# Group norm's product and transposition moved behind the state's renewal in a pooling and RWKV-7 block

## The chip, the cores and the metric

The kernel runs on one core of one Trainium2 chip. The metric is the device time of one execution in microseconds (us), as a median over executions. The engines are TensorE (PE for matmuls, PEld for its weight loads), VectorE (DVE), ScalarE (ACT), GpSimd (POOL) and SyncE (SP), whose queue issues all of the kernel's DMAs.

## What is computed

One layer for a sequence of 4096 tokens with 1024 features. A normalised and modulated input goes through one projection; half of its outputs feed a pooling mixer, the other half an RWKV-7 recurrence with 8 heads of 64; both are gated, put side by side and projected again. The part that matters here is the recurrence and the group norm behind it:

```
def step(S, inp):
    r_t, w_t, k_t, v_t, am_t, b_t = inp
    sa = jnp.einsum('bhij,bhj->bhi', S, am_t)
    S = (S * w_t[:, :, None, :]
         + sa[..., None] * b_t[:, :, None, :]
         + v_t[..., None] * k_t[:, :, None, :])
    y = jnp.einsum('bhij,bhj->bhi', S, r_t)
    return S, y
...
mu = jnp.mean(yh, axis=-1, keepdims=True)
var = jnp.mean(jnp.square(yh - mu), axis=-1, keepdims=True)
yh = (yh - mu) * lax.rsqrt(var + GN_EPS)
yh = yh * ln_w[l].reshape(H, N) + ln_b[l].reshape(H, N)
bonus = jnp.sum(rh * kh * r_k[l].reshape(H, N), axis=-1, keepdims=True) * vh
y_rwkv = (yh + bonus).reshape(B, T, D_RWKV) * jax.nn.silu(z)
```

## The kernel before

Stage one (to about 450 us) prepares the weights and does the pooling half. Stage two handles the recurrence in 16 blocks of 256 tokens, each of four chunks of 64 tokens. A block has three parts, written one behind the other: `scores` (L649) multiplies the chunks' vectors with each other on PE (L663), masks the products on DVE (L670) and copies the diagonal blocks on ACT (L678); `inverse` (L698) turns them over on DVE (L709), scales them and inverts small triangular matrices with some sixty dependent products and sums on DVE (L727, L732); `chain` (L796) walks through the four chunks one after the other. Stage three, the output projection (`project`, L924), runs within and behind the last block.

For one chunk `chain` does this, each step waiting for the one before: PE multiplies the state S with the chunk's vectors (L815); ACT copies the result to xa (L822); PE applies the inverse (L827) and beside it starts the next chunk's sum (`lead`, L790); ACT copies that to UV (L835); PE multiplies it with BT (L843 before, L842 after), which DVE adds to the decayed state: the renewal of S, four products of DVE (L849 before, L848 after; the decay Sd is L839 before, L838 after). Behind it PE finishes the chunk's output (L854), and ACT copies that to y (L861). PE is in order over all of this.

The projections of the next block (`front`, L537: f16 products L557 to L559, their ACT and DVE steps at L561, L562 and behind, the scan L596 among them) are cut into small steps. `fill(n)` issues n of them, so that PE has independent products to do while the chain waits. In the last block the fill is stage three.

The group norm works on two chunks at once, as a generator of three steps: `run(gns[0], 1)` issues one step, `run(gns[0])` all that are left. Step one squares y (ACT, L871), sums (DVE, L873, L874) and takes the power on POOL (L876); step two multiplies y by the result (DVE, L878, called the product below); step three, `gn_out`, transposes y on PE (L890, four transpositions into the tile ytp), scales on ACT (L892, four activations), adds and multiplies on DVE (L893, L894) and stores mx (SP, L896). The first half's steps are issued within the chain, those of the second half in the next block's scores.

The written order isn't the final one. A scheduler orders each engine's instructions by priority, which follows the written order; the products of the chain on PE are kept in their order (`ordered`), and copies and renewals of the chain are raised by 400 places (`tc.high_priority(offset=PRI)`).

Of the kernel before, what the change touches and what calls it, by code (L numbers as in the profile page):

```python
# [52 lines left out]
def kernel(  # L53
# [426 lines left out]
    with ExitStack() as ph:  # L480
# [289 lines left out]
        def ordered(mm):  # L770

            pin[0] = True
            return tc.keep_in_program_order(mm)
# [22 lines left out]
        def chain(b, f, fill):  # L796
            AR, UV, sc, BT, pc = f["AR"], f["UV"], f["sc"], f["BT"], f["pc"]
            MT = UV[0:64].rearrange("q c (h t) -> q (c h) t", h=NH)
            pe, po = f["px"]
            uo = 4 * HS  # L800
            for ch in range(NCH):
                par = 256 * (ch % 2)

                psn = ps_s.tile([P, 512], F32, tag="psn", name=f"psn{b}_{ch}")
                if ch % 2 == 0:
                    y = blk.tile([P, 512], F32, tag="y", name=f"y{b}_{ch}", bufs=3)
                yv = y[64 * (ch % 2) : 64 * (ch % 2) + 64].rearrange("q (j f e) -> q j f e", f=2, e=HS)
                uv = UV[0:64, ch, :].rearrange("q (j f e) -> q j f e", f=2, e=HS)

                for p in range(NPAIR):  # L810
                    cs = slice(par + p * HS, par + (p + 1) * HS)
                    for ar in range(2):
                        for hf, px in ((0, pe), (1, po)):
                            o, ro = 64 * hf, 64 * (hf ^ ar)
                            ordered(PE.matmul(  # L815
                                px[ro : ro + 64, cs], AR[o : o + 64, p, ch, ar, :], S[o : o + 64, p, :],
                                start=(p == 0 and ar == 1), stop=(ar == 0), skip_group_check=True,
                            ))
                xa = blk.tile([64, 2, 256], F32, tag="W", name=f"xa{b}_{ch}")
                for hf, px in ((0, pe), (1, po)):  # L820
                    with tc.high_priority(offset=PRI):
                        A.copy(xa[:, hf, :], px[64 * hf : 64 * hf + 64, par : par + 256])  # L822
                fill(FA)
                nl = lead(b, f, ch + 1) if ch + 1 < NCH else iter(())
                for p in range(NPAIR):
                    for hf in range(2):
                        ordered(PE.matmul(  # L827
                            psn[64 * hf : 64 * hf + 64, uo + p * HS : uo + (p + 1) * HS],
                            MT[:, ch * NH + 2 * p + hf, :], xa[:, hf, p * HS : (p + 1) * HS],
                            start=True, stop=True, skip_group_check=True,  # L830
                        ))
                    run(nl, 1)
                for hf in range(2):
                    with tc.high_priority(offset=PRI):
                        A.copy(uv[:, :, hf], psn[64 * hf : 64 * hf + 64, uo:].rearrange("q (j e) -> q j e", e=HS))  # L835
                run(gns[0], 1)

                Sd = blk.tile([P, NPAIR, HS], F32, tag="Wt", name=f"Sd{b}_{ch}")  # L838
                V.tensor_mul(Sd, S, pc[:, :, ch : ch + 1].to_broadcast([P, NPAIR, HS]))  # L839
                fill(FB)  # L840
                for h in range(NH):
                    o, e = 64 * (h % 2), slice(h * HS, (h + 1) * HS)  # L842
                    ordered(PE.matmul(  # L843
                        psn[o : o + 64, (h // 2) * HS : (h // 2 + 1) * HS], BT[:, ch, e], UV[:, ch, e],
                        start=True, stop=True, skip_group_check=True,
                    ))
                with tc.high_priority(offset=PRI):
                    for p in range(NPAIR):  # L848
                        V.scalar_tensor_tensor(  # L849
                            S[:, p, :], psn[:, p * HS : (p + 1) * HS], pc[:, p, ch : ch + 1], Sd[:, p, :], op0=ALU.mult, op1=ALU.add,  # L850
                        )
                for h in range(NH):
                    hf, o = h % 2, 64 * (1 - h % 2)
                    ordered(PE.matmul(  # L854
                        (pe, po)[hf][o : o + 64, par + (h // 2) * HS : par + (h // 2 + 1) * HS],
                        sc[:, ch * NH + h, 64:128], UV[:, ch, h * HS : (h + 1) * HS],
                        start=False, stop=True, skip_group_check=True,
                    ))
                for hf, px in ((0, pe), (1, po)):
                    o = 64 * (1 - hf)  # L860
                    A.copy(yv[:, :, hf], px[o : o + 64, par : par + 256].rearrange("q (j e) -> q j e", e=HS))  # L861
                run(gns[0])
                if ch % 2 == 1:
                    gns[0] = gn(b, f, ch // 2, y)
                    run(gns[0], 1)
                fill(FY)

        def gn(b, f, j, y):
            bon, szt = f["bon"], f["szt"]
            ysq = blk.tile([P, 512], F32, tag="y", name=f"ysq{b}_{j}", bufs=3)  # L870
            A.activation(ysq, y, AF.Square)  # L871
            var = sm.tile([P, NH], F32, tag="var", name=f"var{b}_{j}")
            V.tensor_reduce(var, ysq.rearrange("q (h j) -> q h j", h=NH), axis=AX.X, op=ALU.add)  # L873
            V.tensor_scalar(var, var, 1.0 / HS, GN_EPS, op0=ALU.mult, op1=ALU.add)  # L874
            rstd = sm.tile([P, NH], F32, tag="rstd", name=f"rstd{b}_{j}")
            G.tensor_tensor(rstd, var, nhalf[:, :NH], op=ALU.pow)  # L876
            yield
            V.tensor_mul(  # L878
                y.rearrange("q (h j) -> q h j", h=NH), y.rearrange("q (h j) -> q h j", h=NH),
                rstd.unsqueeze(2).to_broadcast([P, NH, HS]),  # L880
            )
            yield
            gn_out(b, f, j, y)
# [32 lines left out]
        def run(g, n=100000):  # L916
            for _ in range(n):
                if next(g, run) is run:
                    return
# [48 lines left out]
        gns = [iter(())]  # L968
# [84 lines left out]
```

## Time and profile before

| what | us |
|---|---|
| median of three executions | 2112.47 |
| lowest, highest | 2110.7, 2113.29 |
| the profiled execution | 2114.03 |
| its span, first to last instruction | 2112.3 |
| mean granted clock of TensorE, as a share | 0.984 |

The profiled execution is 1.56 us above the median, and 1.7 us of it lie outside the span. The profile's times count from the start of the span. One row of a timeline is an instruction, or several alike; the brackets at its end give the idle time of the engine ahead of it and what ended it.

### The profile page before, as it was taken

To read this page: it belongs to the slowest core of one execution; us is meant where nothing else is said; L and a number is where in the kernel's file an instruction comes from. 1 tells how busy PE (TensorE), PEld (TensorE's weight loads), DVE (VectorE), ACT (ScalarE), POOL (GpSimd) and SP (SyncE) were. 2 spreads that over 40 slices of the span, in tenths; PEclk is the share of its full clock that TensorE was granted. 3 is DMA by queue.
4 is the path that set the end of the run, shared out by engine and by line. 5 is a ranking of instruction groups with operands and counts; after the bars stand their busy time and mean duration, and the time that the engine had idled before them with its cause. 6 is when DMAs were issued, how large, how long until landed. Compare 5 with 4: busy or idle time off the path is not lost.

```text
span 2112.3 us, 48406 instructions
## 1 busy us (share of the span) xinstructions
PE 1979.8 (94%) x20186; PEld 1460.1 (69%) x20186; DVE 1404.4 (66%) x3533; ACT 1045.7 (50%) x2247; POOL 130.8 (6%) x262
## 2 busy tenths in 40 slices
PE   5999999999999999999999999999999989999998
PEld 2444444687777777777777777777777767788886
DVE  7898987466857757668577676685675766533333
ACT  3555433355565565655655656556556553322211
POOL 0000000000000000000000000000000000100000
PEclk8999999999999999999999999999999999999999
DMA  8867767200110110101101101011011334433422
GB/s 311 277 224 240 241 216 271 68 21 2 32 32 2 31 27 7 32 4 30 32 2 31 27 7 32 3 30 32 2 31 31 131 112 139 165 136 133 155 96 74
DMA packets 140445, 183.20 MB, mean 87 GB/s; under 512 B 12097, under 2 KB 94017, under 8 KB 140226
## 3 DMA queue, kind: packets, MB, share of 16 engines
q1 hardware_dynamic: 140226, 180.11, 25.9%
q8 instruction: 158, 2.59, 0.5%
q14 instruction: 61, 0.50, 0.1%
HBM read 121.22 MB, written 58.85 MB: 85 GB/s over the span
## 4 chain that ended last, share of the span: by engine, by line
PE 47%; DVE 31%; ACT 13%; issue 4%; DMA 2%; POOL 1%; SPq 0%; ACTq 0%; DVEq 0%; POOLq 0%
PE po L953 6%; PE po L955 6%; PE po L954 6%; DVE Wt L727 5%; DVE W L732 4%; PE pp L412 4%; PE pp L411 4%; PE pp L410 4%; PE pj L557 3%; PE pj L558 2%; PE pj L559 2%; DVE sc L670 2%; PE scp_sc L663 2%; DVE L L596 2%; ACT UV L678 2%
## 5 line engine op out<-in xcount | busy, mean ns | idle before, releaser
L557 PE MATMUL pj<-hh,w2h 128*128 128x257 f16 x2176 | 604.3, 278 | 14.3 <-DVE kS L562 13.5
L559 PE MATMUL pj<-hh,w2l 128*128 128x257 f16 x2176 | 598.1, 275 | 0.0
L558 PE MATMUL pj<-hl,w2h 128*128 128x257 f16 x2176 | 596.6, 274 | 0.0
L557 PEld LDWEIGHTS <-w2h 128*128 128x128 f16 x2176 | 213.1, 98 | 69.1 <-issue 27.4
L558 PEld LDWEIGHTS <-w2h 128*128 128x128 f16 x2176 | 215.6, 99 | 47.8 <-issue 17.0
L559 PEld LDWEIGHTS <-w2l 128*128 128x128 f16 x2176 | 211.7, 97 | 31.7
L953 PE MATMUL po<-wo,mh 128*128 128x512 f32 x512 | 204.6, 400 | 2.4 <-ACT mh L937 2.4
L954 PE MATMUL po<-wo,mh 128*128 128x512 f32 x512 | 202.1, 395 | 0.0
L411 PE MATMUL pp<-lo,w1h 128*128 128x512 f16 x512 | 194.0, 379 | 1.4 <-DVE lo L225 1.4
L410 PE MATMUL pp<-hi,w1h 128*128 128x512 f16 x512 | 194.1, 380 | 0.6 <-ACT hi L224 0.6
L412 PE MATMUL pp<-hi,w1l 128*128 128x512 f16 x512 | 194.0, 379 | 0.0
L957 DVE TENSOR_TENSOR x<-po,x 128x512 f32<-128x512 f32 x64 | 44.2, 691 | 155.8 <-PE po L955 155.7
L959 ACT ACTIVATE sq<-x 128x512 f32<-128x512 f32 x64 | 40.4, 631 | 212.0 <-DVE x L957 194.9
L727 DVE TENSOR_TENSOR Wt<-W,Ab 128x30 f32<-128x30 f32 (+7 forms) x480 | 118.5, 247 | 13.7 <-ACT Ab L711 3.1
L732 DVE TENSOR_TENSOR W<-W,Wt 128x30 f32<-128x30 f32 (+7 forms) x480 | 117.9, 246 | 8.8
L953 PEld LDWEIGHTS po<-wo,mh 128*128 128x128 f32 x512 | 97.0, 189 | 24.6 <-ACT mh L937 2.6
L954 PEld LDWEIGHTS po<-wo,mh 128*128 128x128 f32 x512 | 96.8, 189 | 22.2
L678 ACT COPY UV<-sc 32x256 f32<-32x256 f32 x128 | 81.5, 637 | 48.4 <-DVE sc L670 46.3
L955 PE MATMUL po<-wo,ml 128*128 128x512 f32 x256 | 101.6, 398 | 0.0
L562 DVE SCALAR_TENSOR_TENSOR kS<-pj,c,kS 128x256 f32<-128x256 f32 x64 | 30.2, 471 | 103.4 <-ACT kS L561 102.9
L412 PEld LDWEIGHTS <-w1l 128*128 128x128 f16 x512 | 50.1, 98 | 61.6 <-issue 2.0
L410 PEld LDWEIGHTS <-w1h 128*128 128x128 f16 x512 | 50.2, 98 | 59.0 <-issue 0.8
(244 smaller groups left out, 3815.1 us busy)
## 6 DMA issues: line engine op xcount, KB each, us to landing
x<-in_x_dram SPq DMA_DIRECT2D x64, 256.0 KB, 3.1
out_dram<-x SPq DMA_DIRECT2D x64, 256.0 KB, 2.0
xk<-in_xT_dram SPq DMA_DIRECT2D x56, 256.0 KB, 4.1
xt<-in_x_dram SPq DMA_DIRECT2D x28, 512.0 KB, 5.7
wada<-in_w_ada_dram SPq DMA_DIRECT2D x24, 512.0 KB, 6.7
w2raw<-in_w_in_dram SPq DMA_DIRECT2D x17, 512.0 KB, 6.0
hh<-hT_hi SPq DMA_DIRECT2D x32, 257.0 KB, 4.1
hl<-hT_lo SPq DMA_DIRECT2D x32, 257.0 KB, 3.3
```

What stands on the lines that cost most here:

```text
L410: PE.matmul(pp, w1_hi[m][:, k, :], hi, start=(k == 0), stop=False)
L411: PE.matmul(pp, w1_hi[m][:, k, :], lo, start=False, stop=False)
L412: PE.matmul(pp, w1_lo[m][:, k, :], hi, start=False, stop=(k == KT - 1))
L557: unpin(PE.matmul(pp, w2_hi[m][:, k, :], hh[k], start=(k == 0), stop=False))
L558: PE.matmul(pp, w2_hi[m][:, k, :], hl[k], start=False, stop=False)
L559: PE.matmul(pp, w2_lo[m][:, k, :], hh[k], start=False, stop=(k == KT - 1))
L678: A.copy(stg[o : o + 32, :, i8], sc[o : o + 32, i8, o : o + 32].rearrange("q i t -> q t i"))
L727: V.tensor_mul(tmp[:, :n, :k], W[:, r0:, k : k + 1].to_broadcast([P, n, k]), Ab[:, k : k + 1, :k].to_broadcast([P, n, k]),)
L732: V.tensor_add(W[:, r0:, :k], W[:, r0:, :k], tmp[:, :n, :k])
L953: unpin(PE.matmul(po, mh[:, k, ts_], wo[0][k][n], start=(k == 0), stop=False))
L954: PE.matmul(po, mh[:, k, ts_], wo[1][k][n], start=False, stop=False)
L955: PE.matmul(po, (ml[:, k] if b % 2 == 0 else ml[k])[:, ts_], wo[0][k][n], start=False, stop=(k == KT - 1))
```

## The change

The call for step two of the first half moves, in every chunk, from behind the copies L835 to behind the renewal of S. The call for the rest, which ran at the end of each chunk, now stands only in the second and fourth chunk, ahead of the next half's start. So of the first half (chunks one and two), step two is issued in the third chunk behind the renewal, and step three, instead of at the end of the third chunk, in the fourth behind its renewal.

```diff
@@ -833,7 +833,6 @@
                 for hf in range(2):
                     with tc.high_priority(offset=PRI):
                         A.copy(uv[:, :, hf], psn[64 * hf : 64 * hf + 64, uo:].rearrange("q (j e) -> q j e", e=HS))
-                run(gns[0], 1)
 
                 Sd = blk.tile([P, NPAIR, HS], F32, tag="Wt", name=f"Sd{b}_{ch}")
                 V.tensor_mul(Sd, S, pc[:, :, ch : ch + 1].to_broadcast([P, NPAIR, HS]))
@@ -849,6 +848,7 @@
                         V.scalar_tensor_tensor(
                             S[:, p, :], psn[:, p * HS : (p + 1) * HS], pc[:, p, ch : ch + 1], Sd[:, p, :], op0=ALU.mult, op1=ALU.add,
                         )
+                run(gns[0], 1)
                 for h in range(NH):
                     hf, o = h % 2, 64 * (1 - h % 2)
                     ordered(PE.matmul(
@@ -859,8 +859,8 @@
                 for hf, px in ((0, pe), (1, po)):
                     o = 64 * (1 - hf)
                     A.copy(yv[:, :, hf], px[o : o + 64, par : par + 256].rearrange("q (j e) -> q j e", e=HS))
-                run(gns[0])
                 if ch % 2 == 1:
+                    run(gns[0])
                     gns[0] = gn(b, f, ch // 2, y)
                     run(gns[0], 1)
                 fill(FY)
```

On DVE, in the third chunk of a block (the numbers are buffers), this stands from the second renewal to the third in the changed kernel:

```order
L848 SCALAR_TENSOR_TENSOR S<-psn_1_5199,pc_3683,Sd_1_5246 128x64 x4
L838 TENSOR_TENSOR Sd_2_5358<-S,pc_3683 128x256
L873 TENSOR_REDUCE var_0_5288<-ysq_0_5286 128x8
L874 TENSOR_SCALAR var_0_5288<-var_0_5288 128x8
L878 TENSOR_TENSOR y_0_5105<-y_0_5105,rstd_0_5291 128x512
L596 SCALAR_TENSOR_TENSOR L_3_5262<-rst,tw_3_5260 128x256
L608 SCALAR_TENSOR_TENSOR AR_4333<-kS_13_5162,vec,Ppad_3665 128x4x64
L606 SCALAR_TENSOR_TENSOR tb_3_5395<-ta_3_5261,kS_13_5162 128x256
L611 TENSOR_TENSOR AR_4333<-rS_14_5257,Ppad_3665 128x4x64
L609 SCALAR_TENSOR_TENSOR BK_4572<-tb_3_5395,pv,Pi_3_5263 128x4x64
L610 TENSOR_TENSOR ta_3_5261<-ta_3_5261,kS_13_5162 128x256
L848 SCALAR_TENSOR_TENSOR S<-psn_2_5300,pc_3683,Sd_2_5358 128x64 x4
```

The kernel before has these twelve in the same order: the product L878 did not move on its engine.

On DVE, from the third renewal to the fourth (mx is the tile of step three, vS a projection of the next block):

```order
-L615 SCALAR_TENSOR_TENSOR rk_3_5417<-rS_14_5257,pv,ta_3_5261 128x256
-L839 TENSOR_TENSOR Sd_3_5462<-S,pc_3683 128x256
-L893 TENSOR_TENSOR mx_0_5390<-mx_0_5390,bon_3681 128x512
-L562 SCALAR_TENSOR_TENSOR vS_15_5405<-pj_15_5293,c_103,vS_15_5405 128x256
-L894 TENSOR_TENSOR mx_0_5390<-mx_0_5390,szt_3682 128x512
-L849 SCALAR_TENSOR_TENSOR S<-psn_3_5423,pc_3683,Sd_3_5462 128x64 x4
+L562 SCALAR_TENSOR_TENSOR vS_15_5392<-pj_15_5293,c_103,vS_15_5392 128x256
+L615 SCALAR_TENSOR_TENSOR rk_3_5404<-rS_14_5257,pv,ta_3_5261 128x256
+L838 TENSOR_TENSOR Sd_3_5449<-S,pc_3683 128x256
+L848 SCALAR_TENSOR_TENSOR S<-psn_3_5410,pc_3683,Sd_3_5449 128x64 x4
+L893 TENSOR_TENSOR mx_0_5470<-mx_0_5470,bon_3681 128x512
+L894 TENSOR_TENSOR mx_0_5470<-mx_0_5470,szt_3682 128x512
```

L893 and L894 moved from ahead of the fourth renewal to behind it, where L562 of zS, L873, L620, L874 and the first mask L670 follow in this order (before, L873, L562, L874, the mask and then L620 did). On ACT the four L892 moved in the same way, from behind the third chunk's copies L861, ahead of the copies L822, to behind the fourth chunk's copies L835, ahead of its L861.

On PE, around the fourth chunk's product with BT (scp is the next block's score product), before:

```order
L557 LDWEIGHTS w2h_2179
L557 MATMUL pj_16_5419<-hh_1_4329,w2h_2179 128x257
L558 LDWEIGHTS w2h_2179
L558 MATMUL pj_16_5419<-hl_1_4331,w2h_2179 128x257
L559 LDWEIGHTS w2l_2180
L559 MATMUL pj_16_5419<-hh_1_4329,w2l_2180 128x257
L663 MATMUL scp_0_sc<-AR_4333,BK_4572 128x128
L843 MATMUL psn_3_5423<-UV_3684,BT_4310 64x64 x8
L854 MATMUL px_0_5007<-UV_3684,sc_4309 64x64
```

and now:

```order
L557 LDWEIGHTS w2h_2179
L557 MATMUL pj_16_5406<-hh_1_4329,w2h_2179 128x257
L558 LDWEIGHTS w2h_2179
L558 MATMUL pj_16_5406<-hl_1_4331,w2h_2179 128x257
L559 LDWEIGHTS w2l_2180
L559 MATMUL pj_16_5406<-hh_1_4329,w2l_2180 128x257
L890 MATMUL ytp_0_5469<-ident,y_0_5105 128x128
L842 MATMUL psn_3_5410<-UV_3684,BT_4310 64x64 x8
L890 MATMUL ytp_0_5469<-ident,y_0_5105 128x128 x3
L854 MATMUL px_0_5007<-UV_3684,sc_4309 64x64
```

The transpositions L890 stood one ahead of the third chunk's L843 and three behind its L854; there an f16 product (L557) has taken the first one's place. Fifteen blocks are changed alike. In the last block the first half's four transpositions move to behind the fourth chunk's L842, and the second half's four to five output products later. On SP the store L896 of the first half now stands behind the next three loads of hh and hl instead of ahead of them, and POOL's order is the same.

## Rows read from the trace of the kernel before

**Rows 1.** The page: its head and part 1.

```profile
span 2112.3 us, 48406 instructions
...
PE 1979.8 (94%) x20186; PEld 1460.1 (69%) x20186; DVE 1404.4 (66%) x3533; ACT 1045.7 (50%) x2247; POOL 130.8 (6%) x262
```

**Rows 2.** The chain of waits from 604 to 692 us: start, length, what.

```profile
625.32 1.40 ACT mx L892 x4
...
630.58 1.24 DVE Ab L709
...
663.57 0.70 PE pl L591 x2
```

**Rows 3.** Timeline of weight loads, 604.5 to 608.2 us: start, length, instruction, idle before.

```profile
605.54 0.14 PEld L890 LDWEIGHTS ytp<-ident,y 128*128 128x128 f32 x1 [0.39 <-DVE y L878]
607.53 0.55 PEld L843 LDWEIGHTS psn<-UV,BT 128*64 128x64 f32 x16 [1.85 <-ACT UV L835]
```

**Rows 4.** Timeline of weight loads, 608.2 to 620 us.

```profile
608.61 0.31 PEld L890 LDWEIGHTS ytp<-ident,y 128*128 128x128 f32 x3
...
609.75 0.56 PEld L815 LDWEIGHTS px<-S,AR 64*64 64x64 f32 x32 [0.21 <-ACT y L861]
...
611.93 0.54 PEld L827 LDWEIGHTS psn<-xa,UV 64*64 64x64 f32 x14 [0.20 <-ACT xa L822]
...
613.30 0.29 PEld L663 LDWEIGHTS scp_sc<-AR,BK 64*128 64x128 f32 x2 [0.21 <-issue]
613.72 0.55 PEld L843 LDWEIGHTS psn<-UV,BT 128*64 128x64 f32 x16
```

**Rows 5.** Timeline of DVE, 604 to 640 us.

```profile
604.79 0.69 DVE L878 TENSOR_TENSOR y<-y,rstd 128x512 f32<-128x512 f32 x1 [1.75 <-POOL rstd L876]
...
610.90 0.69 DVE L893 TENSOR_TENSOR mx<-mx,bon 128x512 f32<-128x512 f32 x1 [0.57 <-ACT mx L892]
...
611.90 0.68 DVE L894 TENSOR_TENSOR mx<-mx,szt 128x512 f32<-128x512 f32 x1
614.52 0.86 DVE L849 SCALAR_TENSOR_TENSOR S<-psn,pc,Sd 128x64 f32<-128x64 f32 x4 [1.94 <-PE psn L843]
616.35 0.69 DVE L873 TENSOR_REDUCE var<-ysq 128x8 f32<-128x512 f32 x1 [0.97 <-ACT ysq L871]
...
617.42 0.68 DVE L670 TENSOR_TENSOR sc<-scp_sc,mask 128x512 f32<-128x512 f32 x1
618.02 0.42 DVE L620 SCALAR_TENSOR_TENSOR szt<-tz,zS 128x256 f32<-128x256 f32 x1
...
619.26 0.69 DVE L878 TENSOR_TENSOR y<-y,rstd 128x512 f32<-128x512 f32 x1 [0.23 <-POOL rstd L876]
...
622.26 0.69 DVE L670 TENSOR_TENSOR sc<-scp_sc,mask 128x512 f32<-128x512 f32 x1 [1.11 <-PE scp_px L663]
```

**Rows 6.** Timeline of ACT, 604 to 640 us.

```profile
608.72 0.76 ACT L861 COPY y<-px 64x256 f32<-64x256 f32 x2 [0.68 <-PE px L854]
609.38 1.49 ACT L892 ACTIVATE mx<-ytp,pv 128x128 f32<-128x128 f32 x4
...
611.12 0.76 ACT L822 COPY xa<-px 64x256 f32<-64x256 f32 x2
...
621.22 1.28 ACT L678 COPY UV<-sc 32x256 f32<-32x256 f32 x2
...
623.04 0.47 ACT L561 ACTIVATE lo<-pj,c 128x256 f32<-128x256 f32 x1 [0.17 <-PE pj L559]
```

**Rows 7.** Windows: length; busy PE, PEld, DVE, ACT, POOL; granted clock; DMA share, GB/s.

```profile
523.78:530.97 7.19, 7.19 (x110) 5.51 (x108) 3.60 (x11) 4.07 (x11) 0.00 (x0) 0.77 0.20 54
608.41:614.52 6.11, 6.04 (x110) 4.67 (x108) 3.60 (x11) 3.84 (x11) 0.00 (x0) 1.00 0.28 76
...
1706.94:1713.05 6.11, 6.04 (x110) 4.67 (x108) 3.60 (x11) 3.84 (x11) 0.00 (x0) 1.00 0.52 160
...
523.80:527.10 3.30, 3.30 (x51) 2.45 (x46) 2.38 (x9) 2.60 (x7) 0.00 (x0) 0.50 0.00 0
```

## The prediction

> **What bounds the kernel now.** I read the page first: in a span of 2112.3 us TensorE has a matmul in flight for 94% and DVE is busy for 66% [rows 1]. That alone says little, because a busy PE includes its pipeline. So I went to one block of stage two, the second one (block 1, from about 604 us), and read the chain of waits there. It changes engines: from the copies L678 and the activations L892 (625.32) it goes through DVE to the transposition L709 of Ab (630.58), stays on DVE through the sixty products and sums of the inversion, and comes back to PE only at 663.57 [rows 2]. So whatever makes L709 late makes the block late, one for one, while PE can fall behind or run ahead a little in the score stage without any effect. That is the first thing to see: the change touches PE, ACT and DVE just before this stage, and the engine to watch is not PE.
>
> Then I read the place of the change. In the third chunk PE stands still twice: 0.39 us ahead of the first transposition L890, for the product L878, and 1.85 us ahead of L843, for the copy L835 [rows 3]. The first wait is the one that the change takes away. The second has another cause: on DVE the scan L596 stands behind L878, which had itself waited 1.75 us for POOL's power (at 604.79) [rows 5], and ACT's copy L835 stands behind two activations that need the scan.
>
> **What the change does, part by part.**
>
> The product L878. The order of DVE shows it in the same place as before, between L874 and the scan L596, although the code now issues it behind the third renewal. So the 1.75 us that DVE waits for POOL stay, the scan stays late, and the 1.85 us stay. Cost and gain: nothing. Nothing needs to cover it, since no row moved.
>
> The wait of 0.39 us. PE now runs one f16 product instead of the transposition and then waits for the same copy L835. The two waits and the transposition together went from 605.15 (605.54 less 0.39) to 607.53, 2.38 us [rows 3]; now it is one wait, shorter than that by the product, that ends at the same 607.53. The wait that was named goes, and the next one is longer by as much. Gain: nothing.
>
> Behind L842 of the third chunk. Three transpositions and the four activations L892 are gone from here. L815 then waits for the copies of y, which end at 609.48 (608.72 and 0.76) [rows 6], so it starts near 609.55 instead of 609.75 [rows 4]: 0.2 us. ACT no longer has 1.49 us of L892 ahead of the copy L822 (611.12), for whose end L827 waited until 611.93 [rows 4, 6]. Without it L822 runs when L815 is done, near 610.45, and L827's loads need not wait past the end of that copy (0.76 us), so they are through near 611.4 instead of 611.93: 0.5 us in all. The single score product that took from 613.30 to 613.72 [rows 4] is replaced by a transposition of about 0.1 us less. So the fourth chunk's L842 comes about 0.6 us earlier; ends 0.2 (L815 alone) and 0.75 (everything, and the gap ahead of it).
>
> Behind L842 of the fourth chunk. What was taken away arrives here. On DVE the place ahead of the fourth renewal had 1.94 us of idle time [rows 5], so L893 and L894 cost nothing there, and the fourth renewal is not held by them now. But behind it they stand in front of the score masks. I count from L842. L892 takes 1.49 us [rows 6]; it cannot end before 1.8 us (0.3 for the first transposition's result, and 1.49), and not after 2.4 (0.55 for L842's products, 0.31 for three transpositions [rows 4], and 1.49). I take 2.0. Then come L893 and L894, 1.37 us, then the segment from L873 to the first mask, 1.07 us before (616.35 to 617.42), in which L620 (0.42) now stands too [rows 5]. The first mask L670 starts near 4.8 us; before it was 617.42 less 613.72 [rows 4, 5], 3.7 us. That is 1.1 us later. Its cover was the 0.97 us of idle time ahead of L873 [rows 5]; the sum from L842 has no idle time left in it, so that cover is used up. The second half's L878 follows that segment by 1.9 us as before (617.42 to 619.26), since POOL's power stands between [rows 5], so the second chunk's masks and ACT's copy of them, which started at 621.22 [rows 6], are 1.1 to 1.2 us late. Slack left: DVE had 1.11 us of waiting for PE's third scores [rows 5], but ACT, which has that copy in front of it, only 0.17 us ahead of L561 [rows 6]. So ACT comes about 1.0 us late to L892 of the second half and with it L709. Ends: 0.4, if the activations end at 1.8 and half of the rest is hidden, and 1.5, if they end at 2.4.
>
> Net per block: 1.0 late less 0.6 early, **0.4 us later**; fifteen blocks, 6.0 us. Ends: 0.75 early less 0.4 gives 0.35 us earlier (5 us in all), and 1.5 less 0.6 gives 0.9 us later (13 us).
>
> SP's queue. The store of mx now stands behind the next three loads of hh and hl. Nobody waits for that store before the output stage of the last block, so it costs nothing; cover is the whole block. POOL's order does not change.
>
> The last block. Its two sets of transpositions move among output products that have their operands. I book nothing, with one wait like the 1.85 us [rows 3] either way.
>
> The clock. In ten of the fifteen stretches from the third to the fourth renewal the granted clock reads 0.76 to 0.84, in five 1.00; the first of the slow ones lasts 7.19 us and the first of the others 6.11 [rows 7], 1.08 us less. Inside a slow one the clock is at 0.50, the 1.2 GHz level [rows 7], and it falls right behind the stall of [rows 3]. Now the stall is one piece of little under 2.38 us instead of 0.39 and 1.85 with a transposition between, so I expect the fall in no fewer blocks. There can be fifteen at most; I take twelve, two more than before, 2.2 us. Ends: two fewer (2.2 us less), since the blocks' places in time shift too, and five more (5.4 us more).
>
> Sum: 6.0 and 2.2, 8.2 us. Durations come from an execution of 2114.03 us; the runs shown have a median of 2112.47, 1.56 us below. On the median: **2120.7 us**.
>
> **Rivals.**
>
> Faster. The fourth chunk starts 0.6 us earlier, and the masks' delay is swallowed by the 1.11 us that DVE waits for the third scores [rows 5] and by ACT's waits. Then PE and L709 keep the 0.6 us: 9.0 us less, 2103.5 us. It decides at ACT's copy at 621.22 [rows 6]: if its successor's place, relative to L842, is not later by more than 0.6 us, this holds. Against it: the copy has a full queue behind it and 0.17 us of slack. Chance 0.12.
>
> No change. The product did not move, PE's work is the same, and PE's busy share is 94% [rows 1]; if PE's order sets the pace from the third chunk into the scores, what leaves one chunk returns in the next, and the time is 2112.5 us. Against it: the chain leaves PE before L709. Chance 0.22.
>
> Slower by more. PE falls behind too. Ahead of the lone score product stands a gap of 0.21 us with no late input, where PE goes from products of 128 by 128 to those of 64 by 128 [rows 4]. The transpositions, 128 by 128, now stand on both sides of L842, 128 by 64, so two such changes are added in front of products of the chain, 0.42 us per block; if L709 comes to hang on PE's scores, that is 6.3 us on top, 2127.0 us. The Trainium skill has a rule for it, in "TensorEngine Tiling (Array Packing)", section "Key Properties": a change of tiling mode, not of the tile alone, drains TensorE. It speaks against this change; the trace agrees with a gap at that place, and by the rule the sum would be those 2127.0 us, where by the rows the DVE path hides it. Chance 0.10.
>
> **How the numbers follow.** The forecast, 2120.7 us, has 0.56. Its own range goes from 0.15 us per block without any more slow stretches (2114.7) to 0.4 us with five more (6.0 and 5.4, 2123.9): 2115 to 2124 us. About 0.2% (4.2 us) is what a measurement of this kernel can tell from no change. Faster by more than that: 0.12, the first rival. Within: 0.22 and the lower edge of the forecast, 0.06, so 0.28. Slower: 0.50 and 0.10, so 0.60. The range of 2109 to 2127 us leaves out the faster rival and the end above, not more than 2 in 10.
>
> **What would show it.** In the profile after: L878 still directly ahead of L596; one wait ahead of L842 of the third chunk, over 2 us long and for L835; the stretch from third to fourth renewal near 5.5 us at full clock instead of 6.11; the first mask near 4.8 us behind L842 instead of 3.7; L709 near 17.9 us behind the fourth L842 instead of 16.86 (613.72 to 630.58) [rows 2, 4]; more than ten stretches below clock 1.00. The prediction is wrong if L709 keeps its 16.86 us, or if the slow stretches become fewer than eight.

## The result, and the profile after

The changed kernel takes **2128.51 us** (median of four executions, 2127.07 to 2130.46); the kernel before took 2112.88 us on the same chip (four executions, 2110.7 to 2114.73). The ratio is 1.0075 with a 95% interval of 1.0057 to 1.0092: slower, beyond the 0.2% that can be told apart, and 1.5 us above the upper end of the range. The direction was as forecast; the size, 15.6 us, is about twice the 8.2 us of the forecast. In the profiled executions the spans differ by 15.3 us [rows 1]:

```profile
span 2127.6 us, 48413 instructions
...
PE 1989.0 (93%) x20186; PEld 1466.3 (69%) x20186; DVE 1406.5 (66%) x3533; ACT 1048.0 (49%) x2247; POOL 130.0 (6%) x262
```

Where the clock does not fall, all blocks but the last two repeat within 0.2 us and mostly within some hundredths, so the second block stands for them. The third and fourth product behind the copies L835 (L842 here, L843 before) and the transposition L709 cut a block into stretches; I measure them from row to row in both traces:

| stretch, us | before | after |
|---|---|---|
| third to fourth L842, at full clock | 6.19 (5 blocks) | 5.25 (1 block) |
| the same, where the clock falls | 7.27 (10 blocks) | 6.48 (14 blocks) |
| fourth L842 to first mask L670 | 3.70 | 5.55 |
| fourth L842 to the second chunk's masks | 6.16 | 8.00 |
| fourth L842 to L709 | 16.85 | 18.32 |
| L709 to the next block's first L842 | 46.51 | 46.52 |

That is the whole difference. Fourteen blocks gain 0.94 us ahead of the fourth L842 and lose 1.47 behind it, 0.53 each, 7.4 us. The clock costs 14 falls of 1.23 us (6.48 less 5.25) instead of 10 of 1.08, 6.4 us more. The fifteenth block adds 0.6; the last takes as long as before (323.20 us from its first L842 to the end of the span, 323.23 before). The first L842 of all comes 0.8 us later (509.69 us instead of 508.88), which is chance: nothing ahead of it was changed, and in the profiled executions of the experiments it lies between 507.0 and 512.9. Together 15.2 of the 15.3 us. Why the clock falls in four more blocks is a question of its own, and the runs below leave it open.

The timeline of weight loads of the second block, third and fourth chunk; it answers to [rows 3, 4]:

```profile
609.02 0.55 PEld L842 LDWEIGHTS psn<-UV,BT 128*64 128x64 f32 x16 [2.27 <-ACT UV L835]
...
615.16 0.14 PEld L890 LDWEIGHTS ytp<-ident,y 128*128 128x128 f32 x1
615.51 0.55 PEld L842 LDWEIGHTS psn<-UV,BT 128*64 128x64 f32 x16 [0.21 <-ACT UV L835]
616.12 0.31 PEld L890 LDWEIGHTS ytp<-ident,y 128*128 128x128 f32 x3
616.60 0.55 PEld L854 LDWEIGHTS px<-UV,sc 128*64 128x64 f32 x16 [0.17 <-issue]
...
617.99 0.74 PEld L663 LDWEIGHTS scp_sc<-AR,BK 64*128 64x128 f32 x6 [0.21 <-issue]
618.66 0.52 PEld L663 LDWEIGHTS scp_px<-AR,BK 64*128 64x128 f32 x4
```

One stall of 2.27 us has taken the place of 0.39 and 1.85. The transpositions stand around the fourth L842, and the first chunk's scores no longer alternate between their two tiles: six for one, then four for the other.

The windows from the third to the fourth renewal, with the columns of [rows 7]:

```profile
524.58:530.98 6.40, 6.40 (x97) 4.62 (x94) 2.40 (x10) 2.68 (x7) 0.00 (x0) 0.73 0.20 42
609.90:616.30 6.40, 6.40 (x97) 4.61 (x94) 2.40 (x10) 2.68 (x7) 0.00 (x0) 0.73 0.18 44
1721.70:1726.86 5.16, 5.16 (x97) 3.99 (x94) 2.40 (x10) 2.58 (x7) 0.00 (x0) 1.00 0.52 153
```

The second block, at full clock before (608.41 in [rows 7]), is now a slow one; only the window at 1721.70 stayed at 1.00.

DVE, which answers to [rows 5]:

```profile
606.28 0.69 DVE L878 TENSOR_TENSOR y<-y,rstd 128x512 f32<-128x512 f32 x1 [1.75 <-POOL rstd L876]
606.89 0.69 DVE L596 TENSOR_TENSOR_SCAN L<-rst,tw 128x256 f32<-128x256 f32 x1
...
616.30 0.86 DVE L848 SCALAR_TENSOR_TENSOR S<-psn,pc,Sd 128x64 f32<-128x64 f32 x4 [3.56 <-PE psn L842]
618.25 0.69 DVE L893 TENSOR_TENSOR mx<-mx,bon 128x512 f32<-128x512 f32 x1 [1.09 <-ACT mx L892]
618.97 0.69 DVE L894 TENSOR_TENSOR mx<-mx,szt 128x512 f32<-128x512 f32 x1
...
620.05 0.69 DVE L873 TENSOR_REDUCE var<-ysq 128x8 f32<-128x512 f32 x1
...
621.05 0.69 DVE L670 TENSOR_TENSOR sc<-scp_sc,mask 128x512 f32<-128x512 f32 x1
...
622.90 0.69 DVE L878 TENSOR_TENSOR y<-y,rstd 128x512 f32<-128x512 f32 x1 [0.56 <-POOL rstd L876]
623.50 0.68 DVE L670 TENSOR_TENSOR sc<-scp_sc,mask 128x512 f32<-128x512 f32 x1
...
625.35 0.69 DVE L670 TENSOR_TENSOR sc<-scp_sc,mask 128x512 f32<-128x512 f32 x1 [0.56 <-PE scp_px L663]
...
633.83 1.24 DVE L709 STREAM_TRANSPOSE Ab<-UV 64x1024 f32<-64x1024 f32 x1 [1.02 <-ACT UV L678]
```

The first half's L878 still stands directly ahead of the scan and still waits 1.75 us for POOL: the product that the change issues later did not move. In the fourth chunk DVE now waits for L892, does the two adds, and comes to the first mask 5.54 us behind L842 (621.05 less 615.51). But it waits again behind that, for POOL, ahead of the second half's L878. ACT, which answers to [rows 6], shows why:

```profile
616.71 1.51 ACT L892 ACTIVATE mx<-ytp,pv 128x128 f32<-128x128 f32 x4 [1.25 <-PE ytp L890]
618.24 0.76 ACT L861 COPY y<-px 64x256 f32<-64x256 f32 x2
...
619.39 0.62 ACT L871 ACTIVATE ysq<-y 128x512 f32<-128x512 f32 x1
```

The four activations wait for the last of the transpositions and then hold back the copies of y and the second half's square L871, which starts 3.88 us behind L842 instead of 1.97 (615.69 less 613.72 before). The chain of waits passes there, from POOL's power through L878 and the masks to ACT's copies [rows 2]:

```profile
621.23 1.65 POOL rstd L876
622.90 0.69 DVE y L878
623.59 1.21 DVE sc L670 x2
```

(The profile puts POOL's own wait down to a product of PE, L640. The sum L874 is the nearer reason: it ends 0.08 us ahead of POOL's start in both kernels, at 621.15 here and at 617.51 before, where POOL started at 617.59.)

So L878 of the second half is the meeting point of two things that came late: its power, by way of ACT's square, and its place on DVE, behind the adds and the masks. The first experiments ask which of them counts, or whether it is PE, whose third scores come 1.30 us later behind L842 than before (624.16 less 615.51, and 621.07 less 613.72).

### The profile page after: what moved, and what is told of

Same layout as the page of the kernel before. It is cut to its first block, busy times and chain, and to the rows that moved or that the text cites. A ratio compares the mean times of both kernels' runs of the same rounds, so it can differ in the third digit from the quotient of the medians.

```text
span 2127.6 us, 48413 instructions
## 1 busy us (share of the span) xinstructions
PE 1989.0 (93%) x20186; PEld 1466.3 (69%) x20186; DVE 1406.5 (66%) x3533; ACT 1048.0 (49%) x2247; POOL 130.0 (6%) x262
## 4 chain that ended last, share of the span: by engine, by line
PE 47%; DVE 32%; ACT 13%; issue 4%; POOL 2%; DMA 2%; SPq 0%; ACTq 0%; DVEq 0%; POOLq 0%
PE po L953 6%; PE po L955 5%; PE po L954 5%; DVE Wt L727 5%; DVE W L732 4%; PE pp L412 4%; PE pp L411 4%; PE pp L410 4%; PE pj L557 3%; POOL rstd L876 2%; PE pj L558 2%; PE pj L559 2%; ACT UV L678 2%; DVE L L596 2%; DVE sc L670 2%
## 5 line engine op out<-in xcount | busy, mean ns | idle before, releaser
L557 PE MATMUL pj<-hh,w2h 128*128 128x257 f16 x2176 | 606.3, 279 | 14.5 <-DVE kS L562 13.7
L557 PEld LDWEIGHTS <-w2h 128*128 128x128 f16 x2176 | 212.9, 98 | 71.7 <-issue 27.4
L562 DVE SCALAR_TENSOR_TENSOR kS<-pj,c,kS 128x256 f32<-128x256 f32 x64 | 30.1, 471 | 103.2 <-ACT kS L561 102.8
L848 DVE SCALAR_TENSOR_TENSOR S<-psn,pc,Sd 128x64 f32<-128x64 f32 x256 | 54.6, 276 | 59.7 <-PE psn L842 59.7
```

What stands on the lines that cost most here:

```text
L557: unpin(PE.matmul(pp, w2_hi[m][:, k, :], hh[k], start=(k == 0), stop=False))
```

## The experiments

All ratios are against the kernel before, measured beside each run. In each of these traces the fourth renewal starts 0.79 us behind the fourth L842 (616.30 less 615.51), so a renewal's row tells where L842 stood. Renewal, square and the rest carry other line numbers where an edit adds lines.

### The first piece of the change alone

```diff
                 if ch % 2 == 1:
-                    run(gns[0])
+                run(gns[0])
+                if ch % 2 == 1:
                     gns[0] = gn(b, f, ch // 2, y)
```

> Only the first piece of the change: step two of the group norm is issued behind the renewal, and gn_out again runs at the end of every chunk. Every theory: the instructions of each engine stand as in the kernel before, so 2112.9 us (2109 to 2117), the 1.75 us ahead of L878 and the 1.85 us stall of PE unchanged. If it comes out near 2128 us, the place of step two in the code matters in a way that the order of the engines does not show.

Measured: 2114.22 us, ratio 1.0001 (0.9991 to 1.0011); the stall is 1.85 us in every block, L709 16.85 us behind the fourth L842, 11 clock falls. The place of step two in the code does nothing by itself. What happens comes with the second piece, the later gn_out. The second piece alone was not run: there the first piece decides whether gn_out stands ahead of the fourth renewal or behind it.

### The copies of y ahead of the activations

```diff
-                run(gns[0], 1)
+                if ch % 2 == 0:
+                    run(gns[0], 1)
...
-            for p in range(NPAIR):
-                A.activation(mx[:, p, :], ...)
+            with tc.issue_after(f["yc"].ins) if j == 0 else ExitStack():
+                for p in range(NPAIR):
+                    A.activation(mx[:, p, :], ...)
```

(`f["yc"]` is the later copy L861 of the chunk; `issue_after` sets the order on that engine alone.)

> The changed kernel, but in the fourth chunk ACT's two copies of y (L861) are held ahead of the four activations of the first half (L892); the adds stay where they are. Theory A (ACT, DVE and POOL set L709: the second half's square L871 still stands behind the four activations, so L878 of the second half and all behind it stay as late): L709 stays 18.1 to 18.5 us behind the fourth L842, time 2126 to 2131 us. Theory B (PE sets it: in the changed kernel the first chunk's scores cannot pair their two halves since px is released late, and the third scores come 1.30 us later than before): px is released about 0.9 us earlier, the scores pair again, L709 at 17.0 to 17.5 us, time 2109 to 2117 us. Theory C (the forecast: the adds on DVE delay the masks): no change against the changed kernel, 2126 to 2131 us.

Measured: 2123.70 us, ratio 1.0048 (1.0033 to 1.0063), between the expectations. DVE of the second block:

```profile
617.42 0.86 DVE L848 SCALAR_TENSOR_TENSOR S<-psn,pc,Sd 128x64 f32<-128x64 f32 x4 [3.72 <-PE psn L842]
...
625.75 0.68 DVE L670 TENSOR_TENSOR sc<-scp_sc,mask 128x512 f32<-128x512 f32 x1
...
634.77 1.24 DVE L709 STREAM_TRANSPOSE Ab<-UV 64x1024 f32<-64x1024 f32 x1 [1.02 <-ACT UV L678]
```

The scores alternate again, and the third masks come 9.12 us behind L842 (625.75 less 616.63) with no wait for PE, where the changed kernel had 9.84. L709 is at 18.13 us, 0.19 better, as theory A had it. So PE was late, but hardly on the path: theory B falls. What else it gained on the changed kernel is four clock falls fewer (10 instead of 14).

### The adds late

```diff
-                    run(gns[0])
+                    late[0] = gns[0]
                     gns[0] = gn(b, f, ch // 2, y)
...
+                if ch == 2:
+                    with tc.issue_after(mk.ins):
+                        run(late[0])
...
+            yield
             V.tensor_add(mx, mx, bon[:, :, j * P : (j + 1) * P])
```

> The changed kernel, but the two DVE operations L893 and L894 of the first half are held behind the third chunk's masks of the next block; ACT and PE keep their order. Theory C (the forecast: these 1.37 us stand in front of the masks and are handed on): first mask near 4.2 us behind the fourth L842 instead of 5.55, L709 near 17.0 us, time 2108 to 2113 us. Theory A (the second half's square on ACT is what is late, so L873, POOL and L878 keep their places): first mask near 4.2 us, but L878 of the second half still 7.2 to 7.4 us behind L842, L709 at 17.9 to 18.4 us, time 2123 to 2130 us. Theory B (PE's third scores): third masks still 9.6 to 9.9 us behind L842, time 2125 to 2130 us.

Measured: 2130.15 us, ratio 1.0079 (1.0064 to 1.0094). DVE:

```profile
617.07 0.86 DVE L851 SCALAR_TENSOR_TENSOR S<-psn,pc,Sd 128x64 f32<-128x64 f32 x4 [2.48 <-PE psn L845]
...
620.70 0.68 DVE L670 TENSOR_TENSOR sc<-scp_sc,mask 128x512 f32<-128x512 f32 x1
...
621.29 0.68 DVE L876 TENSOR_REDUCE var<-ysq 128x8 f32<-128x512 f32 x1
...
624.13 0.69 DVE L881 TENSOR_TENSOR y<-y,rstd 128x512 f32<-128x512 f32 x1 [1.16 <-POOL rstd L879]
...
633.90 1.24 DVE L712 STREAM_TRANSPOSE Ab<-UV 64x1024 f32<-64x1024 f32 x1 [0.43 <-ACT UV L678]
```

The first mask is 1.13 us earlier (4.42 us behind L842), near the 4.2 of theories A and C, but the product (L881 here) waits 1.16 us for POOL and is no earlier: 7.85 us behind L842, 7.39 in the changed kernel. ACT's square holds it at 7.39 at best, since it starts 3.88 us behind L842 as in the changed kernel; the rest is that the sum (L876 here) now stands behind the first mask. L709 comes 0.69 us earlier, which theory A did not expect, but the stretch behind it is 0.66 us longer (47.18 instead of 46.52), so the block is no shorter. The longer stretch is another effect of this edit: in all runs with the adds late DVE takes the next projection's step of kS (L562) 32.2 us behind L709 instead of 31.0, and the scan L596 behind it 0.65 us later. The forecast's own theory, C, falls: the adds alone are not what costs the time.

### The square ahead of the activations, and the adds late

```diff
                 if ch % 2 == 1:
-                    run(gns[0])
+                    run(gns[0], 1)
+                    late[0] = gns[0]
                     gns[0] = gn(b, f, ch // 2, y)
                     run(gns[0], 1)
+                    with tc.issue_after(f["ysq"].ins):
+                        run(late[0], 1)
```

(The calls are split as in the two runs above; the second half's product is also kept behind the first chunk's masks, its place before.)

> The changed kernel, but in the fourth chunk ACT takes first the copies of y (L861), then the second half's square (L871), and only then the four activations of the first half; the adds are held as in the run with late adds, and the second half's L878 is kept behind the first chunk's masks, as in the kernel before. Theories A and B: what delayed L709 is gone, L709 at 16.6 to 17.2 us behind the fourth L842, and the 0.8 us that the fourth chunk's L842 gained stay, so 1.2 to 1.7 us less per block than the changed kernel: 2103 to 2111 us, a little faster than the kernel before. If the four activations delay the copies of the masks (L678) wherever they stand, L709 stays above 17.6 us and the time above 2116 us.

Measured: **2092.32 us**, ratio 0.9898 (0.9883 to 0.9913), more than expected and faster than the kernel before. DVE:

```profile
614.23 0.86 DVE L852 SCALAR_TENSOR_TENSOR S<-psn,pc,Sd 128x64 f32<-128x64 f32 x4 [2.47 <-PE psn L846]
...
616.08 0.69 DVE L881 TENSOR_REDUCE var<-ysq 128x8 f32<-128x512 f32 x1 [0.99 <-ACT ysq L879]
...
616.88 0.68 DVE L670 TENSOR_TENSOR sc<-scp_sc,mask 128x512 f32<-128x512 f32 x1
...
619.17 0.69 DVE L886 TENSOR_TENSOR y<-y,rstd 128x512 f32<-128x512 f32 x1
...
629.48 1.24 DVE L713 STREAM_TRANSPOSE Ab<-UV 64x1024 f32<-64x1024 f32 x1 [0.43 <-ACT UV L678]
```

The product is back at 5.73 us behind L842 (5.54 before), and L709 at 16.05. The 0.94 us ahead of the fourth L842 are kept. Of the 0.8 us that L709 gained beyond the kernel before, 0.66 come back behind it, as in the run above. And the clock fell in five blocks only (the expectations below count four), though the stall is still 2.27 us: nine falls fewer than in the changed kernel, some 11 us, and that is why it beat its expectation.

### The square ahead of the activations, without the late adds

Is ACT's order the cause alone? Here the adds follow their activations at once.

```diff
-                        run(late[0], 1)
+                        run(late)
```

> The run with the square first (2092.3 us), but with the two adds of the first half (L893 and L894) issued right behind their activations again, so that they stand ahead of the first chunk's masks on DVE. Theory A (ACT's order alone is the cause: the second half's square behind the four activations): what the square-first run gained is kept but for a few tenths per block, L709 at 16.3 to 17.3 us behind the fourth L842, 2094 to 2112 us. Theory D (two delays lie side by side, ACT's square and DVE's adds, each long enough to hold the second chunk's masks alone, so that taking away one gives nothing, as the run with late adds alone showed for the other side): second chunk's masks at 7.6 to 8.3 us, L709 at 17.8 to 18.5 us, 2118 to 2131 us.

Measured: 2121.24 us, ratio 1.0033 (1.0020 to 1.0046), inside the 2118 to 2131 us of theory D. DVE:

```profile
616.47 0.69 DVE L878 TENSOR_REDUCE var<-ysq 128x8 f32<-128x512 f32 x1 [0.99 <-ACT ysq L876]
...
617.86 0.69 DVE L899 TENSOR_TENSOR mx<-mx,bon 128x512 f32<-128x512 f32 x1 [0.50 <-ACT mx L898]
...
619.80 0.68 DVE L670 TENSOR_TENSOR sc<-scp_sc,mask 128x512 f32<-128x512 f32 x1
...
621.00 0.68 DVE L883 TENSOR_TENSOR y<-y,rstd 128x512 f32<-128x512 f32 x1
```

Now the sum L878 is early, and POOL with it: the product L883 waits for nobody. It is late because adds and masks stand ahead of it on DVE, 7.17 us behind L842. L709 is at 17.99. From the fourth L842 to the next block's first, the time is 64.84 us in the changed kernel, 64.81 with the adds late, 64.50 with the square first, and 63.23 with both (63.36 in the kernel before). So the late adds are worth 0.03 us with the square behind the activations and 1.27 with it ahead of them; the early square is worth 0.34 us with the adds ahead of the masks and 1.58 with them late. Either delay alone holds most of the block's loss, so theory A falls with C: they lie side by side.

### Without the stall: the kernel before, the changed kernel, and the square-first kernel

The prediction said that the stall of PE comes from L878 ahead of the scan on DVE and from two activations ahead of L835 on ACT. Here both orders are turned round.

```diff
+            with tc.issue_after(scan[0].ins) if j == 0 else ExitStack():
                 V.tensor_mul(
                     y.rearrange("q (h j) -> q h j", h=NH), ...
...
+                    with tc.issue_after(uvc[0].ins) if uvc[0] else ExitStack():
                         A.activation(Pp[:, :, 1:], c3(L), AF.Exp, bias=0.0, scale=cexp)
                         A.activation(Pi, L, AF.Exp, bias=0.0, scale=-cexp)
```

(`scan[0]` is the last scan L596, `uvc[0]` the last copy L835; the exponentials are issued two steps of the projection later.)

On the kernel before:

> The kernel before, with DVE's product L878 of the first half held behind the scan L596, and ACT's two exponentials L597 and L598 held behind the copy L835, so that nothing late stands ahead of L835. Theory S (PE's stall of 1.85 us ahead of the third L842 is made by these two orders, and the clock falls because of the stall): the stall shrinks to under 0.7 us, the third L842 comes 1.3 to 2.0 us earlier, the stretches below full clock between the third and fourth renewal fall from 10 or 11 to 0 to 3: 2070 to 2092 us. Theory T (the products of AR and BK behind the exponentials come later by the copy's 0.73 us, and hold DVE's renewal or PE's scores, or DVE's chain to L709 is late for another reason): the stall goes but L709 keeps its distance from the second renewal, 2104 to 2116 us.

On the changed kernel:

> The changed kernel with the same two orders as in the run on the kernel before (L878 behind the scan, the exponentials behind L835). Theory S: the stall of 2.27 us shrinks to under 0.7 us and the 14 clock falls go to 0 to 3; the fourth renewal still pays the late masks, so L709 stays 17.9 to 18.5 us behind the fourth L842: 14 falls of 1.23 us and 1.5 to 2.0 us per block less, 2081 to 2097 us, and later than the same edit on the kernel before. Theory T: 2118 to 2130 us. If the falls stay though the stall is gone, the fall has another cause than the stall and the time is 2098 to 2110 us.

On the square-first kernel:

> The square-first run (2092.3 us, four falls) with the same two orders. Theory S: 1.5 to 2.0 us per block and four falls of 1.25 us less: 2057 to 2069 us. Theory T: 2086 to 2096 us.

Measured: 2080.56 us, ratio 0.9842 (0.9825 to 0.9859), on the kernel before; 2085.57 us, 0.9863 (0.9846 to 0.9880), on the changed one; **2061.02 us**, 0.9746 (0.9730 to 0.9762), on the square-first one, the fastest of all. All three lie in the ranges of theory S. ACT in the first of them:

```profile
600.91 0.75 ACT L843 COPY UV<-psn 64x256 f32<-64x256 f32 x2 [0.16 <-PE psn L835]
601.56 0.41 ACT L604 ACTIVATE Ppad<-L 128x256 f32<-128x256 f32 x1
```

Its third L842 (L851 here) in the timeline of weight loads:

```profile
601.71 0.55 PEld L851 LDWEIGHTS psn<-UV,BT 128*64 128x64 f32 x16 [0.34 <-ACT UV L843]
```

The stall is 0.34 us in all three, the third L842 comes 2.04 us earlier behind the first (11.96 us instead of 14.00; on the kernel before 0.47 of it is lost again ahead of the fourth), and no window between third and fourth renewal is below full clock. The changed kernel gains the same 2.04 us and loses 0.59 of it again ahead of the fourth (5.84 us instead of 5.25), but it is rid of 14 falls where the kernel before is rid of 10. It stays slower than the kernel before by the late L709 (18.09 us behind the fourth product, 16.85 there).

### Four buffers

```diff
-                    y = blk.tile([P, 512], F32, tag="y", name=f"y{b}_{ch}", bufs=3)
+                    y = blk.tile([P, 512], F32, tag="y", name=f"y{b}_{ch}", bufs=4)
```

(The same for ysq and mx, which share the tag.)

> The changed kernel with four buffers instead of three behind the tag y, which y, ysq and mx share; every engine keeps its order. Theory W (the four activations L892 of the first half wait for the last transposition because mx takes the buffer of the y that the transpositions read): the first of them starts 0.3 to 1.2 us earlier, the last ends near 2.3 us behind the fourth L842 instead of 2.71, L871 and the first mask come 0.2 to 0.4 us earlier, 0.2 to 0.4 us less per block: 2122 to 2126 us. Theory V (they wait for the last transposition because all four lie in one PSUM tile): no row moves, 2126 to 2131 us.

Measured: 2128.82 us, ratio 1.0071 (1.0054 to 1.0087). ACT:

```profile
614.49 1.50 ACT L892 ACTIVATE mx<-ytp,pv 128x128 f32<-128x128 f32 x4 [1.25 <-PE ytp L890]
```

The fourth L842 of this block starts at 613.28, so the activations start 1.21 us behind it, as in the changed kernel (616.71 less 615.51). The shared buffer is not what they wait for; theory W falls. The semaphore that the first activation waits for is updated, in the trace, by the last of the four transpositions alone. That the common PSUM tile is the reason for this was not tried by itself.

### The product really moved

Here the changed kernel gets only the first of the two orders: L878 behind the scan.

> The changed kernel with the product L878 of the first half really behind the scan L596 on DVE (ACT keeps the exponentials ahead of L835). Theory S1 (half of the stall is the scan's wait behind L878, half the two exponentials ahead of L835): the scan starts 0.7 to 0.8 us earlier, the stall ahead of the third L842 is 1.4 to 1.6 us instead of 2.27, 0.7 to 0.8 us less per block; with as many clock falls as the changed kernel (14) 2116 to 2119 us, with none 2097 to 2102 us. Theory S2 (the exponentials alone make the stall, the scan is ready no earlier): no row moves, 2126 to 2131 us.

Measured: 2100.51 us, ratio 0.9933 (0.9918 to 0.9948), faster than the kernel before. DVE:

```profile
604.38 0.69 DVE L598 TENSOR_TENSOR_SCAN L<-rst,tw 128x256 f32<-128x256 f32 x1 [1.52 <-ACT tw L597]
604.99 0.67 DVE L881 TENSOR_TENSOR y<-y,rstd 128x512 f32<-128x512 f32 x1
```

The third L842 (L844 here) among the weight loads:

```profile
606.52 0.55 PEld L844 LDWEIGHTS psn<-UV,BT 128*64 128x64 f32 x16 [1.44 <-ACT UV L837]
```

The window from the third to the fourth renewal:

```profile
607.40:612.56 5.16, 5.16 (x97) 3.99 (x94) 2.40 (x9) 2.58 (x7) 0.00 (x0) 1.00 0.22 51
```

The scan waits for ACT alone and the product for nobody. The stall is 1.44 us, and the clock does not fall once. A block takes 2.04 us less than in the changed kernel (83.28 instead of 85.32 from third L842 to third L842): 0.82 by the shorter stall, 1.23 by the fall that is gone, in the 14 blocks that had one. L709 keeps its 18.32 us. So a product that really moves on DVE makes the kernel faster than before. Here it moves behind the scan only, still ahead of the third renewal (607.40); the place behind the renewal, which the change names, was not tried.

## Why the prediction came out as it did

The forecast added 8.2 us, the spans differ by 15.3. Of the 7 us between, the clock makes 4.2 (6.4 us where 2.2 were booked), the blocks 2.0 (8.0 where 6.0 were booked), and the chance at the start 0.8.

- **What bounds the kernel.** Right from the masks on: the chain still goes through them, ACT's copies and L709, and L709 to the next block kept its 46.5 us. That PE can fall behind in the score stage without any effect was too strong. In the kernel before, the third masks wait 1.11 us for PE's third scores [rows 5], and the chain of waits comes to them from PE. The change put a later chain in its place, through ACT's square, POOL and L878.
- **L878 does not move; its wait, the late scan and the stall stay.** Right, and shown from both sides: the first piece alone changes nothing, and with the product really moved the ratio is 0.9933.
- **The wait of 0.39 us gives nothing.** Right. The single stall is 2.27 us, inside the 2.38 us that the two waits and the transposition took.
- **The fourth chunk's L842 0.6 us earlier.** Too low: 0.94, beyond the upper end of 0.75. At full clock (the block at 1721.70) L815 starts 1.74 us behind the third L842 (1722.56 less 1720.82) instead of 2.22 [rows 3, 4], 0.48 where 0.2 was booked, and the last stretch ahead of L842 gave 0.26 where 0.1 was booked; the piece between gave 0.20 of its 0.3.
- **The delay behind the fourth L842.** This step failed, in two places. "I take 2.0" for the end of the four activations: they ended 2.71 us behind L842 (618.22 less 615.51), since they all wait for the last transposition, and start 0.28 us behind the end of its weight load (616.43 to 616.71), in which its product runs (to 616.67); even the upper end, 2.4, left that out. The rest of that sum held: from the activations' end to the first mask it booked 2.8 us, and 2.83 were measured. And the mechanism was half of it: the prediction followed DVE alone, and let the second half's L878 trail the masks. ACT's square behind the four activations is a second delay of much the same length beside it: with the adds late alone L878 still comes 7.85 us behind L842, with the square first alone 7.17, and only with both 5.73. L709 came 1.47 us later, not 1.0, just within the end of 1.5.
- **Net per block 0.4 us, 6.0 us in all.** 0.53, 7.4 us in fourteen blocks, and 8.0 with the fifteenth. Both terms were too small, and the errors partly cancelled.
- **Twelve slow stretches instead of ten, 2.2 us.** This step failed by more: fourteen, and each dearer (1.23 instead of 1.08 us), 6.4 us. The four more lie inside the five that the range allowed for, but their price lies above its 5.4 us, since the ten old falls got dearer too. The direction, no fewer falls, was right, but the runs do not bear out its reason, the longer stall: with the same stall of 2.27 us the clock fell in 5 to 14 blocks.
- **SP, POOL, the last block: nothing.** Right for SP, which does not appear in the chain of the stretch, and for the last block; the 0.6 us lie in the fifteenth. POOL's order and its 1.65 us are as before, but it stands in the chain now, because its input comes late.
- **The rivals.** The faster one was to decide at ACT's copy of the second chunk's masks, at 0.6 us: it came 1.81 us later behind L842 (9.31 instead of 7.50) [rows 6]. No change: in the changed kernel PE does not set the pace behind the fourth chunk; the late adds, put on top of the square-first order, moved the ratio from 1.0033 to 0.9898 with the same products on PE (six fewer clock falls are some 7 us of that). Slower by more, PE's gaps: one came with no late input, 0.17 us ahead of L854; the 0.21 us ahead of the fourth L842 end 0.05 us behind the copy L835 (615.46), as the long stall ahead of the third does (608.97, 609.02), so it is that copy that ended them. PE's third scores fell back by 1.30 us, but giving PE 0.7 us of that back moved L709 by 0.19. The Trainium skill's rule in "TensorEngine Tiling (Array Packing)", section "Key Properties", that a change of tiling mode drains TensorE, fits the gap of 0.17 us; the time that the prediction drew from it, 2127.0 us, came close for another reason, by luck. The shapes in the rows do not tell by themselves where such a gap comes: L683, 128 by 64, follows a load of 128 by 128 within 0.01 us (622.73 before).

## What to carry to other kernels

Work that is moved to a later place is paid for on the engine where it lands, and there not only by what it takes, but by what it stands in front of: read the order of every engine at the new place, ACT's as well as DVE's, and look for the first later instruction where two of them meet. If a delay has two causes side by side, taking away one shows little; only the run without both prices them. And look first whether the instruction that a change names moves at all in its engine's order.

## What the runs showed of the hardware

Between the third and the fourth renewal the clock fell to 0.50, the 1.2 GHz level, only behind the long stall of PE, but the stall does not settle it. With one of 1.85 us it fell in 10 and 11 of 15 blocks, with one of 2.27 us in 14, 14, 12, 11, 10 and 5, in kernels whose PE, DVE and ACT run the same instructions in the same order from the second renewal to the end of the stall; with 1.44 us and 0.34 us in none. A fall costs 1.0 to 1.3 us here. The length of one stall is no limit either: near the end of stage two, in the run without the stall on the kernel before, the clock falls at 1690.4 us behind three waits of the weight loads of 1.48, 0.48 and 1.37 us. Which blocks it takes, these runs don't show, so a forecast should carry all of them as its range.

Scores that alternate between their two tiles load faster than one tile behind the other: the sixteen of a chunk took 0.97 us, first load to last (the second chunk of the second block, 618.43 to 619.40 before), and 1.63 us for the first chunk's sixteen in the changed kernel, in six, four, two and four (617.99 to 619.62). In both a load on one tile starts 0.11 us behind the one before it; alternating, one starts on each tile in that time. The six come first there because the second tile, scp_px, waits for ACT: its first load, at 618.66, follows the first copy L861 of px (to 618.61). The Trainium skill says in the same section, "Key Properties", that different tiles can load and multiply in parallel; the trace agrees.
